# Group norm's remainder in the first chunk, two products exchanged, low-rank products two units later

## The chip, the cores and the metric

The kernel runs on one core of a Trainium2 chip. The metric is the device time of one execution in microseconds (us). A core has a matrix engine (PE in the profile; PEld is its loading of weights), a vector engine (DVE), a scalar engine (ACT), a general engine (POOL) and a queue that issues transfers (SP). Each engine takes its instructions in the order in which they were queued. The matrix engine writes only to PSUM, which has eight banks; the vector and the scalar engine read results from there.

## The reference

One layer of a hybrid network over 4096 tokens of width 1024: a causal pooling branch and an RWKV-7 branch read the same normalised input through one projection, and both go into one output projection. The change lies in the RWKV branch.

```python
h = _rmsnorm(x, norm_g[l]) * (1.0 + scale[:, None, :]) + shift[:, None, :]
p = h @ w_in[l]
...
seg = seg + (prev - seg) * mu_shift[l].astype(f32)
r, w_lo, k, v, a_lo, z = jnp.split(seg, split_idx, axis=-1)
w_raw = w0[l] + jnp.tanh(w_lo) @ w_up[l].astype(f32)        # low-rank product 1
w_raw = -jax.nn.softplus(-w_raw) - 0.5
decay = jnp.exp(-jnp.exp(w_raw))
a = jax.nn.sigmoid(a0[l] + a_lo @ a_up[l].astype(f32))      # low-rank product 2
kk = (k * k_k[l]).reshape(B, T, H, N)
kk = kk / jnp.maximum(jnp.linalg.norm(kk, axis=-1, keepdims=True), L2_EPS)
k = k * (1.0 + (a - 1.0) * k_a[l])
yh = _rwkv7_scan(rh, decay, kh, vh, kk, a)                  # S_t = S_{t-1}(diag(w) - kk^T(a kk)) + v^T k
mu = jnp.mean(yh, axis=-1, keepdims=True)
var = jnp.mean(jnp.square(yh - mu), axis=-1, keepdims=True)
yh = (yh - mu) * lax.rsqrt(var + GN_EPS)                    # group norm
yh = yh * ln_w[l].reshape(H, N) + ln_b[l].reshape(H, N)
bonus = jnp.sum(rh * kh * r_k[l].reshape(H, N), axis=-1, keepdims=True) * vh
y_rwkv = (yh + bonus).reshape(B, T, D_RWKV) * jax.nn.silu(z)
```

## The kernel before

A first phase (8 stretches of 512 tokens) makes the pooling branch and writes the normalised input to memory. The second phase, which the change is in, walks over 16 blocks of 256 tokens; a block has four chunks of 64 tokens and eight heads in four pairs `p`. A last phase (`project`) makes the output projection, and fills the last block too.

For each block, `scores` (L649) makes the triangular score matrices of the four chunks, `inverse` (L698) inverts their unit triangular parts by a long sequence of small vector instructions (`Wt` L727 and `W` L732, 30 steps of two), and `chain` (L796) carries the state from chunk to chunk. Between these dependent steps `fill(n)` runs `n` units of `front` (L537) of the next block. A unit is one of the eight k-steps of a projection: three matmuls of 257 columns (L557 to L559). A projection (`seg`) is evicted from PSUM by one ACT and one DVE instruction (L561, L562). `front` makes one projection `lo` and then, for each pair `p`, four: `kS`, `rS`, `vS`, `zS`. After `vS` a row of vector instructions (L606 to L615) makes the operands of the scores of the next block and `rk`, the factor of the bonus.

Three kinds of small work are put between the units of a projection, by the list `mid`, whose key is the unit before which one of them is taken:

- `lowrank` (L588), key 3, so in `vS(p)`: two products `pl`, `pa` (L591, L592), three ACT instructions, the DVE scan `L` (L596), and two exponentials (L597, L598). What is made of `vS(p)` by L608 and later needs these.
- `cent` (L622), key 6: `v` is centred and transposed, `vps` (L625), and copied by two ACT instructions (L627). It needs `vS(p)` alone.
- `bonus` (L632), key 6: a product `pb` of `rk` (L634) and a DVE multiplication `bon` (L635). It needs `rk(p)`.

`cent(p)` is taken in `kS(p+1)`, `bonus(p)` in `rS(p+1)`. Those of the last pair stay over: they and `norms` (L637, the norms of the keys) make the list `todo`, from which `scores` takes one in each of the chunks 0, 1 and 3. In chunk 2 it makes `d2` of the norms.

All these results lie in one pool of PSUM, `ps_pj`, of three banks: `kS`, `vps`, `rS`, `pb`, `vS`, `pl`, `pa`, `zS` follow one another in it, and a product waits until the reader of an earlier one has set a bank free. The scores, the transposed group norm result and the transposed keys (`btp`, L719) share another pool of two banks, `ps_sc`.

The group norm of half a block, `gn` (L868), has three parts: squares, variance and a power on POOL (L871 to L876); `y` times that (L878); and `gn_out` (L885): four transposes `ytp` (L890), four ACT instructions (L892), two DVE instructions (L893, L894) and the transfer of `mx`. For the first half they are spread over chunk 2 of `chain`; for the second half the first part runs at the end of `chain`, the second after chunk 0 of the next block's `scores`, and the third after chunk 2.

The order of the instructions is the written one only in part. A planner at compile time takes, for each engine, what it believes ready, the earlier written first and some parts (`high_priority`: the steps of the inverse, the copies `xa` L822 and `UV` L835, the state's update L849) ahead of others. The matmuls of `chain` and the first one of a projection behind them are pinned to the written order (`ordered`, `unpin`).

Of the kernel before, what the change touches and what calls it, by code (L numbers as in the profile page):

```python
# [52 lines left out]
def kernel(  # L53
# [426 lines left out]
    with ExitStack() as ph:  # L480
# [56 lines left out]
        def front(b, f):  # L537
# [7 lines left out]
                    hx += [ht[:, k, :] for k in range(4)]  # L545


            mid = {3: [], 6: []}

            def seg(m, name, bufs=2):  # L550
                pp = ps_pj.tile([P, TB2 + 1], F32, tag="pj", name=f"pj{b}_{m}")
# [25 lines left out]
            for p in range(NPAIR):  # L577
# [19 lines left out]
                    A.activation(Pp[:, :, 1:], c3(L), AF.Exp, bias=0.0, scale=cexp)  # L597
                    A.activation(Pi, L, AF.Exp, bias=0.0, scale=-cexp)  # L598

                mid[3].append(lowrank)  # L600
                yield
                vS = yield from seg(3 + 4 * p, "vS")
                if p == 0:
# [36 lines left out]
                        PE.matmul(pn[32 * q : 32 * q + 32, :], hsel, sqs[q], start=True, stop=True)  # L640
                    A.copy(ssb, pn)

                mid[6] += [cent, bonus]
                if p < NPAIR - 1:
                    yield
            f["todo"] = [norms] + mid[6]
# [2 lines left out]
        def scores(b, f, fill):  # L649
            AR, BK = f["AR"], f["BK"]  # L650

            d2 = sm.tile([64, NI], F32, tag="d2", name=f"d2_{b}")
            d2T = sm.tile([P, 32], F32, tag="d2T", name=f"d2T{b}")
            sc = blk.tile([P, NI, P], F32, tag="sc", name=f"sc{b}")
            BT = blk.tile([P, NCH, 512], F32, tag="BT", name=f"BT{b}")
            stg = f["stg"] = f["UV"][0:64].rearrange("q c e -> q (c e)")[:, 0:1024].rearrange("q (t i) -> q t i", t=32)
            for ch in range(NCH):

                pts = [pool.tile([P, 512], F32, tag=tg, name=f"scp{b}_{ch}_{tg}") for pool, tg in ((ps_sc, "sc"), (ps_x, "px"))]
                for j in range(4):  # L660
                    for hq in range(2):
                        o = 64 * hq
                        PE.matmul(  # L663
                            pts[hq][:, j * P : (j + 1) * P],
                            BK[o : o + 64, j, ch].rearrange("q a t -> q (a t)"),
                            AR[o : o + 64, j, ch].rearrange("q a t -> q (a t)"),
                            start=True, stop=True,
                        )
                for hq in range(2):
                    V.tensor_mul(  # L670
                        sc[:, ch * NH : (ch + 1) * NH, :].rearrange("q (j h) t -> q j h t", h=2)[:, :, hq],
                        pts[hq].rearrange("q (j t) -> q j t", j=4),
                        mask.unsqueeze(1).to_broadcast([P, 4, P]),
                    )

                for kb in range(2):
                    o, i8 = 32 * kb, slice(ch * NH, (ch + 1) * NH)
                    A.copy(stg[o : o + 32, :, i8], sc[o : o + 32, i8, o : o + 32].rearrange("q i t -> q t i"))  # L678
                fill(FS + 1)
                if ch == 2:  # L680
                    pt = ps_sc.tile([P, 512], F32, tag="sc", name=f"d2p{b}")
                    for c_ in range(NCH):
                        PE.transpose(pt[:64, c_ * P : (c_ + 1) * P], ssb[:, c_ * C : (c_ + 1) * C], ident)
                    V.tensor_scalar_max(
                        d2.rearrange("q (c p h) -> q c p h", c=NCH, h=2),
                        pt[:64].rearrange("q (c p e) -> q c p e", c=NCH, e=32)[:, :, :, 0:2], L2_EPS * L2_EPS,
                    )
                    V.reciprocal(d2, d2)
                    for g in range(2):
                        V.transpose(d2T[64 * g : 64 * g + 64], d2)  # L690
                if ch != 2:
                    f["todo"].pop(0)()
                fill(FS)
                if ch % 2 == 0:
                    run(gns[0], 1)
            f["sc"], f["BT"], f["d2T"] = sc, BT, d2T

        def inverse(b, f, fill):  # L698
# [217 lines left out]
        def run(g, n=100000):  # L916
            for _ in range(n):
                if next(g, run) is run:
                    return
# [48 lines left out]
        gns = [iter(())]  # L968
        fs = {0: {}}
        run(front(0, fs[0]))  # L970
        for b in range(NB2):
            f = fs[b]
            nf = fs[b + 1] = {}
            gf = front(b + 1, nf) if b + 1 < NB2 else iter(())
            fill = lambda n, gf=gf: run(gf, n)
            scores(b, f, fill)
            if b == NB2 - 1:
                gp = itertools.chain(*(project(q) for q in range(NB2)))
                fill = lambda n: run(gp, math.ceil(n * PF))
            inverse(b, f, fill)  # L980
            chain(b, f, fill)
            run(gf)
            if b + 2 == NB2 or NB2 == 1:
                load_wo()
# [68 lines left out]
```

## Time and profile before

| | us |
|---|---|
| time, median of 3 runs | 2112.47 (2110.7 to 2113.29) |
| the profiled execution's own time | 2114.03 |
| its span, first to last instruction | 2112.3 |
| first scores of block 0 to those of block 15 | 447.7 to 1711.8 |
| one block, three lengths in turn | 83.5, 84.6, 84.6 |
| PE busy, share of the span | 94% |
| DVE busy | 66% |
| ACT busy | 50% |
| granted PE clock, mean | 0.984 |

A matmul's duration in the trace includes the time in which it is pipelined with its neighbours, so a row of 257 columns shows 0.27 us while the next one starts 0.11 us later. Busy time of PE is therefore no measure of what it could do; what counts are the waits between the matmuls, and the distance of their starts. A granted clock of 1.00 is 2.4 GHz and one of 0.5 is 1.2 GHz.

### The profile page before, as it was taken

The numbers are of one execution on the slowest core, as the hardware profiler recorded it, in microseconds if no ns is written. First come the engines' busy times: TensorE is split into PE (matmuls) and PEld (weight loads), VectorE is DVE, ScalarE is ACT, GpSimd is POOL, SyncE is SP. The second block draws the span as 40 slices with busy tenths as digits, with TensorE's granted clock in tenths as the row PEclk, the third lists the DMA queues.
The fourth block names the chain that finished last, engine by engine and source line by source line (L and its number), as shares of the span: only waits on it lengthen the run. The fifth ranks groups of instructions, "written<-read, shape, count | busy, mean of one in ns | idle before, by whom it ended". The sixth has DMA issues, their size and how long they took to land.

```text
span 2112.3 us, 48406 instructions
## 1 busy us (share of the span) xinstructions
PE 1979.8 (94%) x20186; PEld 1460.1 (69%) x20186; DVE 1404.4 (66%) x3533; ACT 1045.7 (50%) x2247; POOL 130.8 (6%) x262
## 2 busy tenths in 40 slices
PE   5999999999999999999999999999999989999998
PEld 2444444687777777777777777777777767788886
DVE  7898987466857757668577676685675766533333
ACT  3555433355565565655655656556556553322211
POOL 0000000000000000000000000000000000100000
PEclk8999999999999999999999999999999999999999
DMA  8867767200110110101101101011011334433422
GB/s 311 277 224 240 241 216 271 68 21 2 32 32 2 31 27 7 32 4 30 32 2 31 27 7 32 3 30 32 2 31 31 131 112 139 165 136 133 155 96 74
DMA packets 140445, 183.20 MB, mean 87 GB/s; under 512 B 12097, under 2 KB 94017, under 8 KB 140226
## 3 DMA queue, kind: packets, MB, share of 16 engines
q1 hardware_dynamic: 140226, 180.11, 25.9%
q8 instruction: 158, 2.59, 0.5%
q14 instruction: 61, 0.50, 0.1%
HBM read 121.22 MB, written 58.85 MB: 85 GB/s over the span
## 4 chain that ended last, share of the span: by engine, by line
PE 47%; DVE 31%; ACT 13%; issue 4%; DMA 2%; POOL 1%; SPq 0%; ACTq 0%; DVEq 0%; POOLq 0%
PE po L953 6%; PE po L955 6%; PE po L954 6%; DVE Wt L727 5%; DVE W L732 4%; PE pp L412 4%; PE pp L411 4%; PE pp L410 4%; PE pj L557 3%; PE pj L558 2%; PE pj L559 2%; DVE sc L670 2%; PE scp_sc L663 2%; DVE L L596 2%; ACT UV L678 2%
## 5 line engine op out<-in xcount | busy, mean ns | idle before, releaser
L557 PE MATMUL pj<-hh,w2h 128*128 128x257 f16 x2176 | 604.3, 278 | 14.3 <-DVE kS L562 13.5
L559 PE MATMUL pj<-hh,w2l 128*128 128x257 f16 x2176 | 598.1, 275 | 0.0
L558 PE MATMUL pj<-hl,w2h 128*128 128x257 f16 x2176 | 596.6, 274 | 0.0
L557 PEld LDWEIGHTS <-w2h 128*128 128x128 f16 x2176 | 213.1, 98 | 69.1 <-issue 27.4
L558 PEld LDWEIGHTS <-w2h 128*128 128x128 f16 x2176 | 215.6, 99 | 47.8 <-issue 17.0
L559 PEld LDWEIGHTS <-w2l 128*128 128x128 f16 x2176 | 211.7, 97 | 31.7
L953 PE MATMUL po<-wo,mh 128*128 128x512 f32 x512 | 204.6, 400 | 2.4 <-ACT mh L937 2.4
L954 PE MATMUL po<-wo,mh 128*128 128x512 f32 x512 | 202.1, 395 | 0.0
L411 PE MATMUL pp<-lo,w1h 128*128 128x512 f16 x512 | 194.0, 379 | 1.4 <-DVE lo L225 1.4
L410 PE MATMUL pp<-hi,w1h 128*128 128x512 f16 x512 | 194.1, 380 | 0.6 <-ACT hi L224 0.6
L412 PE MATMUL pp<-hi,w1l 128*128 128x512 f16 x512 | 194.0, 379 | 0.0
L957 DVE TENSOR_TENSOR x<-po,x 128x512 f32<-128x512 f32 x64 | 44.2, 691 | 155.8 <-PE po L955 155.7
L959 ACT ACTIVATE sq<-x 128x512 f32<-128x512 f32 x64 | 40.4, 631 | 212.0 <-DVE x L957 194.9
L727 DVE TENSOR_TENSOR Wt<-W,Ab 128x30 f32<-128x30 f32 (+7 forms) x480 | 118.5, 247 | 13.7 <-ACT Ab L711 3.1
L732 DVE TENSOR_TENSOR W<-W,Wt 128x30 f32<-128x30 f32 (+7 forms) x480 | 117.9, 246 | 8.8
L953 PEld LDWEIGHTS po<-wo,mh 128*128 128x128 f32 x512 | 97.0, 189 | 24.6 <-ACT mh L937 2.6
L954 PEld LDWEIGHTS po<-wo,mh 128*128 128x128 f32 x512 | 96.8, 189 | 22.2
L678 ACT COPY UV<-sc 32x256 f32<-32x256 f32 x128 | 81.5, 637 | 48.4 <-DVE sc L670 46.3
L955 PE MATMUL po<-wo,ml 128*128 128x512 f32 x256 | 101.6, 398 | 0.0
L562 DVE SCALAR_TENSOR_TENSOR kS<-pj,c,kS 128x256 f32<-128x256 f32 x64 | 30.2, 471 | 103.4 <-ACT kS L561 102.9
L412 PEld LDWEIGHTS <-w1l 128*128 128x128 f16 x512 | 50.1, 98 | 61.6 <-issue 2.0
L410 PEld LDWEIGHTS <-w1h 128*128 128x128 f16 x512 | 50.2, 98 | 59.0 <-issue 0.8
(244 smaller groups left out, 3815.1 us busy)
## 6 DMA issues: line engine op xcount, KB each, us to landing
x<-in_x_dram SPq DMA_DIRECT2D x64, 256.0 KB, 3.1
out_dram<-x SPq DMA_DIRECT2D x64, 256.0 KB, 2.0
xk<-in_xT_dram SPq DMA_DIRECT2D x56, 256.0 KB, 4.1
xt<-in_x_dram SPq DMA_DIRECT2D x28, 512.0 KB, 5.7
wada<-in_w_ada_dram SPq DMA_DIRECT2D x24, 512.0 KB, 6.7
w2raw<-in_w_in_dram SPq DMA_DIRECT2D x17, 512.0 KB, 6.0
hh<-hT_hi SPq DMA_DIRECT2D x32, 257.0 KB, 4.1
hl<-hT_lo SPq DMA_DIRECT2D x32, 257.0 KB, 3.3
```

Of the source, the lines that this page charges most:

```text
L410: PE.matmul(pp, w1_hi[m][:, k, :], hi, start=(k == 0), stop=False)
L411: PE.matmul(pp, w1_hi[m][:, k, :], lo, start=False, stop=False)
L412: PE.matmul(pp, w1_lo[m][:, k, :], hi, start=False, stop=(k == KT - 1))
L557: unpin(PE.matmul(pp, w2_hi[m][:, k, :], hh[k], start=(k == 0), stop=False))
L558: PE.matmul(pp, w2_hi[m][:, k, :], hl[k], start=False, stop=False)
L559: PE.matmul(pp, w2_lo[m][:, k, :], hh[k], start=False, stop=(k == KT - 1))
L678: A.copy(stg[o : o + 32, :, i8], sc[o : o + 32, i8, o : o + 32].rearrange("q i t -> q t i"))
L727: V.tensor_mul(tmp[:, :n, :k], W[:, r0:, k : k + 1].to_broadcast([P, n, k]), Ab[:, k : k + 1, :k].to_broadcast([P, n, k]),)
L732: V.tensor_add(W[:, r0:, :k], W[:, r0:, :k], tmp[:, :n, :k])
L953: unpin(PE.matmul(po, mh[:, k, ts_], wo[0][k][n], start=(k == 0), stop=False))
L954: PE.matmul(po, mh[:, k, ts_], wo[1][k][n], start=False, stop=False)
L955: PE.matmul(po, (ml[:, k] if b % 2 == 0 else ml[k])[:, ts_], wo[0][k][n], start=False, stop=(k == KT - 1))
```

## The change

The low-rank products are taken before unit 5 of `vS` and not before unit 3. `bonus` and `cent` change places, so that `bonus(p)` is taken in `kS(p+1)` and `cent(p)` in `rS(p+1)`, and in `todo` the last pair's bonus stands before its `cent`. `scores` takes two of `todo` (`norms` and the bonus) in chunk 0, one (`cent`) in chunk 1 and none later. After chunk 0 the group norm runs to its end, so that its third part moves from chunk 2 to chunk 0.

```diff
-            mid = {3: [], 6: []}
+            mid = {5: [], 6: []}
...
-                mid[3].append(lowrank)
+                mid[5].append(lowrank)
...
-                mid[6] += [cent, bonus]
+                mid[6] += [bonus, cent]
...
-                if ch != 2:
+                for _ in range((2, 1, 0, 0)[ch]):
                     f["todo"].pop(0)()
                 fill(FS)
-                if ch % 2 == 0:
-                    run(gns[0], 1)
+                if ch == 0:
+                    run(gns[0])
```

## Rows read from the trace of the kernel before

**Rows 1.** The page's first part: each engine's busy us, share, instructions.
```profile
PE 1979.8 (94%) x20186; PEld 1460.1 (69%) x20186; DVE 1404.4 (66%) x3533; ACT 1045.7 (50%) x2247; POOL 130.8 (6%) x262
```

**Rows 2.** Windows, two blocks: length; busy PE, PEld, DVE, ACT, POOL; granted clock; DMA, GB/s.
```profile
1288.20:1372.80 84.60, 78.81 (x1061) 62.63 (x1060) 58.61 (x167) 50.08 (x116) 5.94 (x11) 0.98 0.08 21
1372.80:1456.40 83.60, 77.78 (x1062) 61.87 (x1061) 58.59 (x167) 49.98 (x116) 5.94 (x11) 1.00 0.08 22
```

**Rows 3.** Waits of PE, blocks 0 to 14: us in total, times, longest.
```profile
PE psn L843 <- ACT UV L835: 24.9, 15, 1.7
...
PE btp L719 <- ACT BT L720: 17.4, 15, 1.2
PE pj L557 <- DVE kS L562: 13.5, 14, 1.0
...
PE pa L592 <- DVE rS L562: 13.0, 29, 0.5
...
PE pl L591 <- DVE bon L635: 8.8, 29, 0.3
```

**Rows 4.** Timeline around chunk 2 of `chain`: start, us, instruction, [idle before, releaser].
```profile
1363.23 0.69 DVE L878 TENSOR_TENSOR y<-y,rstd 128x512 f32<-128x512 f32 x1 [1.75 <-POOL rstd L876]
1363.84 0.68 DVE L596 TENSOR_TENSOR_SCAN L<-rst,tw 128x256 f32<-128x256 f32 x1
...
1364.55 0.42 ACT L597 ACTIVATE Ppad<-L 128x256 f32<-128x256 f32 x1 [1.59 <-DVE L L596]
...
1365.18 0.73 ACT L835 COPY UV<-psn 64x256 f32<-64x256 f32 x2
...
1365.96 0.69 PE L843 MATMUL psn<-UV,BT 128*64 128x64 f32 x16 [1.66 <-ACT UV L835]
```

**Rows 5.** Windows: the stretch behind that wait, columns as in rows 2.
```profile
1367.80:1370.40 2.60, 2.60 (x41) 1.79 (x40) 1.69 (x5) 2.12 (x6) 0.00 (x0) 0.53 0.00 0
```

**Rows 6.** Timeline of PE: the low-rank products of pair 3, in `chain`.
```profile
1361.00 0.48 PE L591 MATMUL pl<-lo,up 64*128 64x256 f32 x1
1361.01 0.48 PE L592 MATMUL pa<-lo,up 64*128 64x256 f32 x1
...
1361.63 0.28 PE L557 MATMUL pj<-hh,w2h 128*128 128x257 f16 x1
```

**Rows 7.** Timeline of PE: the low-rank products of pairs 0 and 1.
```profile
1309.79 0.70 PE L591 MATMUL pl<-lo,up 64*128 64x256 f32 x2
1310.86 0.70 PE L592 MATMUL pa<-lo,up 64*128 64x256 f32 x2 [0.38 <-DVE rS L562]
...
1323.49 0.70 PE L591 MATMUL pl<-lo,up 64*128 64x256 f32 x2 [0.32 <-DVE bon L635]
1324.71 0.70 PE L592 MATMUL pa<-lo,up 64*128 64x256 f32 x2 [0.52 <-DVE rS L562]
```

**Rows 8.** Timeline: pair 0's scan and `rk`, then `vps` of pairs 0, 1.
```profile
1312.73 0.68 DVE L596 TENSOR_TENSOR_SCAN L<-rst,tw 128x256 f32<-128x256 f32 x1
...
1317.77 0.48 DVE L615 SCALAR_TENSOR_TENSOR rk<-rS,pv,ta 128x256 f32<-128x256 f32 x1
...
1317.81 0.61 PE L625 MATMUL vps<-cmat,vS 128*128 128x128 f32 x4
...
1331.66 0.61 PE L625 MATMUL vps<-cmat,vS 128*128 128x128 f32 x4
```

**Rows 9.** Timeline of `scores`: chunk 1's first product; `y`; group norm's sum; chunk 3's copies.
```profile
1293.31 0.37 PE L663 MATMUL scp_sc<-AR,BK 64*128 64x128 f32 x1
...
1294.14 0.69 DVE L878 TENSOR_TENSOR y<-y,rstd 128x512 f32<-128x512 f32 x1 [0.23 <-POOL rstd L876]
...
1301.61 0.69 DVE L893 TENSOR_TENSOR mx<-mx,bon 128x512 f32<-128x512 f32 x1 [1.77 <-ACT mx L892]
...
1304.13 1.28 ACT L678 COPY UV<-sc 32x256 f32<-32x256 f32 x2 [2.56 <-DVE sc L670]
```

**Rows 10.** Windows: the inverse, columns as in rows 2; timeline: its last transpositions.
```profile
1305.40:1338.10 32.70, 29.47 (x241) 24.11 (x241) 31.07 (x98) 17.26 (x38) 1.64 (x7) 1.00 0.01 3
...
1334.31 2.11 DVE L745 STREAM_TRANSPOSE UV<-W 64x512 f32<-64x512 f32 x2
```

## The prediction

> **What bounds the kernel now.** I read the page first: PE is busy for 94% of the span, no other engine for more than 66% [rows 1]. So PE is the engine to watch, and what can be gained is its waits. The windows of two neighbouring blocks show how regular the second phase is: 84.6 and 83.6 us with the same instructions, the longer one at a mean clock of 0.98 and the shorter at 1.00 [rows 2]. Then the list of PE's waits over blocks 0 to 14: the same few waits come once in each block [rows 3]. Per block they are 1.66 us before the product L843 of chunk 2 (24.9 by 15), 1.16 us before a `btp` (17.4 by 15), 0.97 us before `vS(2)` (13.5 by 14), and about 0.45 us for each `pa` of pairs 0 and 1 and 0.30 us for each `pl` of pairs 1 and 2. The change touches the neighbourhood of every one of them. I therefore went to the timeline around each, and last to the inverse, where DVE is busy for 31.07 of 32.7 us [rows 10]: there PE can't run ahead of DVE by much, whatever is taken out of its way.
>
> The sum is per block and times 15 (blocks 0 to 14 run with a `front` between their steps). It is made against the profiled execution's 2114.03 us, of which 2112.3 is the span and 1.7 lies around it; the median of the runs is 2112.47, so 1.6 comes off at the end.
>
> **Low-rank products, chain (pair 3).** Today they lie before the product L827 of chunk 2. The chain of the 1.66 us wait is written out in [rows 4]: `y` waits for the power on POOL, the scan stands behind `y` on DVE, ACT waits 1.59 us for the scan in front of the exponential L597, and the copy `UV` L835, whose input has been there, is queued behind that exponential; PE's L843 waits for the copy. Two units later the products come behind L827, since the five units before unit 5 are used up by then. The copies L835 are then ready before `tw` and `ta` exist, and stand ahead of the exponentials. What is late next is the scan itself, which now lies beside the state's update L849 and the copies of the next step. I take 1.4 of the 1.66 (bounds 0 and 1.66).
>
> The wait has a second price. In the stretch behind it the granted clock is 0.53 for 2.6 us [rows 5], the lower of the two levels (1.2 GHz), and matmuls that start every 0.11 us elsewhere start at half that pace. In every third block it stays high: that is the difference of 84.6 and 83.6 [rows 2]. Two blocks of three times 1.0 are 0.7 per block, which go with the wait.
>
> **Low-rank products, pairs 0 to 2, and the bonus one projection earlier.** These two must be taken together. Today pair 0 needs 1.07 us from `pl` to `pa`, since `pa` waits for `rS` to leave its bank, and pair 1 0.32 and 1.22 [rows 7]. Where both banks are free, as in pair 3, the two products run side by side and cost 0.63 in all (1361.00 to 1361.63) [rows 6]. Two units later both banks should be free. If nothing else came in, pair 0 would save 1.07 and pair 1 1.22 + 0.32 = 1.54.
>
> But the bonus needs `rk`, `cent` doesn't. For pair 0, counted from the place where `pl` stands now (1309.79): `vps` starts at 8.02, which is 1.07 + 0.63 + 19 units of 0.333 [rows 7, 8]. After the change the same place is reached at 0.67 (two units) + 0.63 + 17 x 0.333 = 6.96, and `pb` stands there. `rk` ends 5.52 after the scan begins (1312.73 to 1318.25), and the scan begins 1.87 after `pa` [rows 7, 8]; with the products at 0.67 that is 0.67 + 1.87 + 5.52 = 8.06. So `pb` waits 1.1 us for `rk`, and the place is passed at 8.06 where it is 8.02 now: nothing gained. In pair 1 the place is 1331.66 - 1323.49 + 0.32 = 8.49 now [rows 7, 8], and 8.06 after: 0.43 gained. Pair 2's bonus falls into the chain, long after its `rk`. Together 0.4 less. The bounds are 2.6 less, if the planner lets units pass the waiting `pb`, and 1.75 more, if `rk` ends 0.67 later than it does now (9.13 against 8.02 and 8.49).
>
> The waiting `pb` holds up everything behind it on PE, the units above all. The Trainium skill (TensorE: Matmul & The Clock Gate, Part 3) says that matmuls start and end strictly in the order of the queue. No row here shows one passing another that waits, so the trace agrees; only the planner's order at compile time could let the units pass, and by the rule the wait of 1.1 us is paid in full where it places `pb` early.
>
> In pair 2, `vS` waits 0.97 for `kS`, whose eviction stands behind the transpositions L745 (2.11 us) [rows 3, 10], and `pl` 0.30. `vS` will have the bank of the bonus to choose as well, and the inverse begins earlier (next part), so the transpositions fall earlier against PE. I take 0.8 less of 1.27; both ends stay open, since DVE is full there.
>
> **Group norm and the bonus in `scores`.** Chunk 3 now pays for the third part in chunk 2: the sum L893 waits 1.77 for ACT in front of chunk 3's masks, the copies L678 of chunk 3 wait 2.56 for those masks, and the copies of `btp` stand behind them on ACT [rows 9]; hence the 1.16 us of `btp`. With the third part in chunk 0, chunk 3 has only its own masks, so I take 1.0 less (bounds 0 and 1.16; the copy L711 of the inverse, now earlier, may come in between). In chunk 0, `y` ends at 1294.83, while PE is at chunk 1's first product at 1293.31 [rows 9]: up to 1.5 us of waiting for the four transposes, if they are queued ahead of chunk 1. The 1.77 of L893 moves too, and can hold chunk 1's masks; behind those PE has three units (1.0) before chunk 2 wants a bank, so up to 0.8. I take 0.6 more between 0 and 2.3, near the low end, since the planner has chunk 1's products to put ahead. The work itself only changes its place. The bonus of pair 3 in chunk 0 has its `rk` since the chain and frees its bank before `cent` in chunk 1. On SP the store of `mx` moves forward with the third part, and stands behind the loads of the next `front`, with nothing queued that waits for it. POOL's queue keeps its order.
>
> **The sum.** -1.4 - 0.7 - 0.4 - 0.8 - 1.0 + 0.6 = -3.7 per block, times 15 is -55.5: 2058.5 against the profiled execution, 2057 against the median.
>
> **The rivals.**
> 1. The planner lets units pass `pb`, so pairs 0 and 1 gain their 2.6: -5.9 per block, 2024. For it: it orders by what it believes ready. Against it: its belief may run ahead of the chip, where `pl` and `pa` were queued 0.3 to 0.5 too early [rows 7].
> 2. The chain's wait only changes its place: the scan, later now, holds `y`'s copies or `xa` instead of `UV`, and the clock falls as before. -0.4 there in place of -2.1: 2082.
> 3. Slower: `rk` slips. DVE is at 95% in the inverse [rows 10], and a scan that comes two units later ends `rk` 0.67 later than now. Then `pb` waits 9.13 - 6.96 = 2.17 in pairs 0 and 1, longer than the 1.66 after which the clock fell [rows 4, 5], so that 0.7 more goes in each. Pairs 0 and 1 give +1.75 + 1.4 in place of -0.4, pair 2's 0.8 is lost with DVE's delay: +0.65 per block, 2122. It decides from about 2 us of wait at each `pb`; with `scores` at its bad end too it is 2148.
> 4. The changed text does not change the queues where it matters (the planner floats the steps back to where their inputs are ready), or gains and losses cancel: 2112.
>
> **How the numbers follow.** Forecast 2057 with 0.55 (its own range 2035 to 2080), rival 1 0.15, rival 2 0.12, rival 3 0.13, rival 4 0.05. Faster by over 0.2% (4 us, about what a measurement of this kernel can tell) is 0.82, within it 0.05, slower 0.13. The range reaches from below rival 1, whose bounds go on to 2012, to 2108; rival 3 and most of rival 4 lie outside.
>
> **What would show it.** Right: L843 of chunk 2 starts without a wait for L835 and no block shows the clock of 0.53 behind it; all `pl` and `pa` pairs at 0.63; the second `btp` wait gone; `pb` of pairs 0 and 1 waiting about 1 us for `rk`; blocks of about 80.6 us. Wrong: waits of over 2 us at `pb`; transposes or masks in chunk 0 and 1 that hold PE by more than 1 us; new waits at `xa` or S in chunk 3; a changed order of the planner anywhere that brings waits the trace of before doesn't have.

## The result, and the profile after

| | before | after |
|---|---|---|
| median time, us | 2112.88 (4 runs) | 2144.72 (2139.36 to 2145.66) |
| ratio to before, 95% interval | | 1.0146 (1.0126 to 1.0165) |
| the profiled execution's own time, span | 2114.03, 2112.3 | 2145.66, 2143.9 |
| mean block, first scores of block 0 to those of block 15 | 84.28 | 86.54 |

The change makes the kernel 1.5% slower; 2057 us had been forecast, with 2108 as the upper end. The engines' totals tell nothing of it; the first part of the page after:

```profile
PE 1994.5 (93%) x20186; PEld 1469.6 (69%) x20186; DVE 1413.7 (66%) x3533; ACT 1041.4 (49%) x2247; POOL 126.4 (6%) x262
```

The list of PE's waits over blocks 0 to 14 does (us in total, times, longest); it answers to [rows 3]:

```profile
PE qp L756 <- DVE MQ L746: 48.8, 15, 3.3
PE pb L634 <- DVE rk L615: 25.6, 15, 1.7
PE psn L827 <- ACT xa L822: 8.7, 30, 0.4
PE pa L592 <- DVE rS L562: 5.3, 15, 0.4
PE ytp L890 <- DVE y L878: 4.9, 14, 0.4
...
PE psn L843 <- ACT UV L835: 0.4, 1, 0.4
```

The waits of [rows 3] are nearly all gone: before L843 24.9 us have become 0.4, and those before `btp` and before `vS` of pair 2 are not in the list. In their place stand 48.8 us before `qp`, 3.25 per block, and 25.6 us before `pb`, 1.7 per block. The first of these no rival had named.

The timeline of block 5 shows what `qp` waits for. First PE (start, us, instruction, idle before, releaser), then DVE in the same stretch:

```profile
921.80 0.28 PE L559 MATMUL pj<-hh,w2l 128*128 128x257 f16 x1
925.32 0.43 PE L756 MATMUL qp<-MQ,sc 32*32 32x32 f32 x26 [3.24 <-DVE MQ L746]
925.78 0.45 PE L634 MATMUL pb<-rk,bones 128*128 128x256 f32 x1
```

```profile
920.66 0.69 DVE L743 TENSOR_TENSOR W<-W,d2T 128x512 f32<-128x512 f32 x1
921.26 0.42 DVE L610 TENSOR_TENSOR ta<-ta,kS 128x256 f32<-128x256 f32 x1
921.60 2.07 DVE L745 STREAM_TRANSPOSE UV<-W 64x512 f32<-64x512 f32 x2
923.70 0.43 DVE L612 TENSOR_TENSOR BK<-ta,Pi 128x256 f32<-128x256 f32 x1
924.04 1.23 DVE L746 STREAM_TRANSPOSE MQ<-UV 32x1024 f32<-32x1024 f32 x1
925.20 0.43 DVE L615 SCALAR_TENSOR_TENSOR rk<-rS,pv,ta 128x256 f32<-128x256 f32 x1
925.56 0.47 DVE L562 SCALAR_TENSOR_TENSOR zS<-pj,c,zS 128x256 f32<-128x256 f32 x1
925.96 0.46 DVE L562 SCALAR_TENSOR_TENSOR kS<-pj,c,kS 128x256 f32<-128x256 f32 x1
```

The closing steps of the inverse (L743 to L746) hold DVE from 920.66 to 925.27, with two short instructions of pair 1 (L610, L612) between them, and the eviction of `zS` of pair 1, then that of `kS` of pair 2, come behind them. `kS(2)` is complete on PE at about 922.1, and the next projection has no bank. The planner has filled the hole with the first 26 products of `qp`, which need the last of the closing steps. The same stretch of DVE in the kernel before, a part that [rows 10] cut short:

```profile
1331.58 0.48 DVE L615 SCALAR_TENSOR_TENSOR rk<-rS,pv,ta 128x256 f32<-128x256 f32 x1
...
1332.08 0.47 DVE L562 SCALAR_TENSOR_TENSOR zS<-pj,c,zS 128x256 f32<-128x256 f32 x1
...
1333.38 0.68 DVE L743 TENSOR_TENSOR W<-W,d2T 128x512 f32<-128x512 f32 x1
...
1336.46 0.48 DVE L562 SCALAR_TENSOR_TENSOR kS<-pj,c,kS 128x256 f32<-128x256 f32 x1
```

There `rk(1)` and the eviction of `zS(1)` come before L743. Only `kS(2)` stands behind a part of the closing steps, and it is wanted one projection later; that was the 0.97 us before `vS(2)` [rows 3], a wait that is gone after the change.

Counted from the first score product of block 5, in us (unit n is the n-th unit queued on PE in the block; unit 82 begins `rS(2)`):

| | before | after | difference |
|---|---|---|---|
| inverse begins (L709) | 17.25 | 16.48 | -0.77 |
| unit 30 | 23.64 | 21.72 | -1.92 (the low-rank products not yet done) |
| unit 48 | 30.06 | 29.48 | -0.58 |
| unit 50 (after pair 0's wait) | 30.73 | 32.52 | +1.80 |
| unit 80 | 43.91 | 43.67 | -0.23 |
| closing steps begin (L743) | 45.17 | 43.08 | -2.09 |
| unit 82 | 44.57 | 48.71 | +4.14 |
| unit 110 (start of the chain) | 60.35 | 63.31 | +2.96 |
| next block's first scores | 83.53 | 85.27 | +1.74 |

Up to unit 80 the change is worth 0.23 us; between units 80 and 82, 4.37 us are lost; behind it some 2.4 come back, where pair 2 waited before and in the chain. Of the 4.37, 3.24 are the wait. Most of the rest is work that stands there now, the 26 products of `qp` and `pb`, and stood elsewhere before.

### The profile page after: what moved, and what is told of

The parts are those of the page before. It is cut to its first block, busy times and chain, and to the rows that moved or that the text cites. A ratio compares the mean times of both kernels' runs of the same rounds, so it can differ in the third digit from the quotient of the medians.

```text
span 2143.9 us, 48451 instructions
## 1 busy us (share of the span) xinstructions
PE 1994.5 (93%) x20186; PEld 1469.6 (69%) x20186; DVE 1413.7 (66%) x3533; ACT 1041.4 (49%) x2247; POOL 126.4 (6%) x262
## 4 chain that ended last, share of the span: by engine, by line
PE 49%; DVE 29%; ACT 9%; issue 9%; DMA 2%; POOL 1%; SPq 0%; ACTq 0%; POOLq 0%; DVEq 0%
PE po L953 6%; PE po L955 5%; PE po L954 5%; DVE W L732 5%; DVE Wt L727 5%; PE pp L412 4%; PE pp L411 4%; PE pp L410 4%; PE pj L557 3%; PE pj L558 3%; PE pj L559 3%; DVE L L596 2%; DVE sc L670 2%; PE pb L634 2%; PE psn L827 2%
## 5 line engine op out<-in xcount | busy, mean ns | idle before, releaser
L562 DVE SCALAR_TENSOR_TENSOR rS<-pj,c,rS 128x256 f32<-128x256 f32 x64 | 30.8, 481 | 136.0 <-ACT rS L561 136.0
```

## The experiments

The difference has three parts, so I first ran each part and each pair of parts alone. The parts are L (low-rank products at unit 5), X (the exchange) and G (group norm and the list `todo`).

**L with G: `low_gn`.** The changed kernel with

```diff
-                mid[6] += [bonus, cent]
+                mid[6] += [cent, bonus]
```

> The changed kernel with the exchange alone undone: the centring comes first again, the bonus one projection later; low-rank products at unit 5 and group norm in chunk 0 stay. Theory A (the bonus stands ahead of its factor rk, and the two long waits of PE, 1.78 us before pair 0's bonus product and 3.32 us before the early part of qp, both come from that): both waits go, the gains at L843, btp and vS(2) stay, about 80.7 us per block and 2060 us. Rival B (the planner pulls qp forward because the inverse begins earlier with group norm in chunk 0, whatever the bonus does): the 3.3 us stay, only the 1.78 goes, about 2118 us. Rival C (the low-rank products two units later are what delays the rest): no faster than 2130 us.

Measured: 2139.16 us, 1.0122 (1.0105 to 1.0139). Theory A falls: without the exchange the kernel is nearly as slow. Rival B's wait before `qp` is there, though the time is 21 us above its figure, and rival C's bound is met as well; the next runs tell these two apart. PE's waits:

```profile
PE qp L756 <- DVE MQ L746: 45.5, 15, 3.0
PE pj L557 <- DVE zS L562: 18.2, 15, 1.2
```

And in place of the bonus product, the projection `rS(1)` waits 1.2 us, for the eviction of `zS` of pair 0.

**L with X: `low_swap`.** The changed kernel with

```diff
-                for _ in range((2, 1, 0, 0)[ch]):
+                if ch != 2:
                     f["todo"].pop(0)()
                 fill(FS)
-                if ch == 0:
-                    run(gns[0])
+                if ch % 2 == 0:
+                    run(gns[0], 1)
```

> The changed kernel with group norm and the list todo as before (third part in chunk 2, one of todo in chunks 0, 1 and 3); low-rank products at unit 5 and the exchange stay. Theory A: the bonus still stands ahead of rk, so PE still waits some 5 us per block for it, and the btp wait of 1.2 us comes back for the 0.5 us at the transposes: about 2150 us. Rival B (earlier inverse): the 3.3 us before qp are gone, about 2105 us. Rival C: as now, about 2145 us.

Measured: 2098.83 us, 0.9926 (0.9909 to 0.9942). Near rival B's figure: without G the kernel is faster than before, though `pb` still waits (28.0 us put down to `rk` and 21.1 us to the steps of the inverse queued around it). Theory A and rival C had it as slow as the whole change.

**`qp` kept in place: `after_qp_pinned`.**

```diff
-                    PE.matmul(pt[32 * q : 32 * q + 32, j * 32 : (j + 1) * 32], sc[0:32, i, 32:64], MQ[0:32, i, :], start=True, stop=True)
+                    ordered(PE.matmul(pt[32 * q : 32 * q + 32, j * 32 : (j + 1) * 32], sc[0:32, i, 32:64], MQ[0:32, i, :], start=True, stop=True))
```

> The changed kernel with the 32 matmuls of qp (L756) pinned to the written order on PE, so that none of them is queued ahead of the units written before it. Theory A: the 3.3 us are pair 1's bonus product waiting for rk, with qp only standing in front of it; it waits for rk itself now, and the time is within 15 us of the changed kernel's, 2130 to 2145 us. Rival B: qp queued early is itself the wait, which goes: 3.3 us less per block, about 2095 us.

Measured: 2150.81 us, 1.0176 (1.0161 to 1.0191). No faster than the change, and far from rival B's 2095: `qp` queued early only stands in front of the hole. The wait passes to the bonus product, whose `rk` is behind the closing steps too, as theory A had it; the next run shows that `rk` is not the last thing in the way.

```profile
PE pb L634 <- DVE rk L615: 77.6, 29, 3.7
```

**No wait for `rk`: `after_bonus_no_rk`.** The bonus term of the output is left out by it.

```diff
-                    PE.matmul(pb, bones, rk, start=True, stop=True)
+                    PE.matmul(pb, bones, vS, start=True, stop=True)
```

> The changed kernel with the bonus product reading vS in place of rk: the same instructions of the same size, but nothing waits for rk (the bonus term of the output is left out so). Theory A: neither the 1.78 us before pair 0's bonus product nor the 3.3 us before qp are left, about 2060 us. Rival B: only the first goes, about 2118 us. Rival C: the waits for pa and the late scan stay, no faster than 2130 us.

Measured: 2140.13 us, 1.0126 (1.0111 to 1.0141). With nothing waiting for `rk` the time hardly falls. The wait before `qp` is 45.7 us in 15 blocks, 3.05 each, and the wait of pair 0 has become one for the eviction of `zS` (18.3 us, 15 times). In block 5, `rS(2)` then starts at 48.35 from the block's first scores, and the eviction of `zS(1)` ends at 48.30. So the bonus is not what holds the kernel; both waits are for work that is late on DVE.

**Each part alone.** `only_low`, `only_swap` and `only_gn` are the kernel before with the lines of L, X or G; `swap_gn` has X and G.

> The kernel before with one part of the change: low-rank products before unit 5. Theory A (only the exchange does harm): the 1.9 us before L843 of chunk 2 and most of the clock lost behind it go, and pl and pa wait less: about 3 us less per block, 2068 us. Rival C (the later low-rank products do the harm): slower than before, about 2130 us.

Measured: 2077.36 us, 0.9835 (0.9819 to 0.9852), which no run beats beyond its interval, and within 10 us of the expectation. The wait before L843 is gone and every block takes 82.0 us.

> The kernel before with one part of the change: bonus and centring exchanged (in the list todo too). Theory A: pairs 0 and 1 wait for rk, about 0.5 to 1.5 us each, with the low-rank products still at unit 3, and the other waits stay: about 2135 us. Rival B (harm only together with the earlier inverse): within 10 us of before, 2113 us.

Measured: 2132.85 us, 1.0096 (1.0079 to 1.0113), near theory A's figure, with waits of 0.37 and 0.43 at `pb` and longer ones at the low-rank products.

> The kernel before with one part of the change: group norm's remainder in chunk 0, and the list todo taken two, one, none, none (its order stays centring, then bonus). Theory A: the btp wait of 1.2 us goes and 0.5 us at the transposes comes, about 2103 us. Rival B (the earlier inverse makes the planner queue qp too early): a new wait before qp, about 2140 us.

Measured: 2125.01 us, 1.0058 (1.0042 to 1.0074): slower, though the `btp` wait is gone. The new wait is not at `qp` but at `rS(2)`, for the eviction of `zS`:

```profile
PE pj L557 <- DVE zS L562: 27.0, 15, 1.8
```

> The changed kernel with the low-rank products back before unit 3; exchange and group norm in chunk 0 stay. Theory A: rk ends two units earlier, so the bonus waits are smaller but there, and the 1.9 us before L843 and the clock lost behind it come back: about 2135 us. Rival C (the later low-rank products do the harm): no slower than before, about 2105 us.

Measured: 2123.41 us, 1.0051 (1.0036 to 1.0066), between the two expectations.

So L alone gains, and G costs in three companies of four: 1.0058 alone, 1.0122 against 0.9835 beside L, 1.0146 against 0.9926 beside L and X; beside X alone it is 1.0051 against 1.0096. All the kernels with G have a wait at unit 82, none of those without it has. That gave theory D: G lets the inverse begin 0.77 us earlier and end earlier still, and its closing steps, which have priority, get ahead of the evictions. The next four runs test it.

**Closing steps without priority: `after_tail_plain`.** The changed kernel with

```diff
             MQ = blk.tile([P, NI, 32], F32, tag="Ab", name=f"MQ{b}")
-            with tc.high_priority(offset=PRI):
+            if True:
                 for kb in range(2):
...
                 V.tensor_mul(W, W, d2T.unsqueeze(1).to_broadcast([P, 16, 32]))
```

> The changed kernel with the closing steps of the inverse (L743 to L748: a product, three transpositions, a copy) at ordinary priority and not ahead of all else. Theory D, formed from the runs so far (group norm in chunk 0 lets the inverse end some 2 us earlier, and its closing steps, 4.6 us on DVE, are now queued ahead of the evictions of zS of pair 1 and kS of pair 2 and of rk of pair 1; PE has no bank and waits 3.3 us): the evictions go first, the 3.3 us wait goes, about 2095 us. Rival E (the wait is for the result of the inverse itself, which PE reaches too early): the result comes later still, so the wait stays or grows, no faster than 2140 us.

Measured: 2085.62 us, 0.9867 (0.9851 to 0.9884): 59 us faster than the change, and faster than before. Per mean block that is 4.04 us (86.54 against 82.50). In block 5, whose clock is full in both, it is 2.58; the rest is for the most part the lower clock of other blocks, which is gone: every block behind block 0 takes 82.7 to 83.0. The DVE timeline of block 5 shows the new order; `rk` and `zS` come between L743 and the transpositions:

```profile
902.57 0.69 DVE L743 TENSOR_TENSOR W<-W,d2T 128x512 f32<-128x512 f32 x1
903.51 0.48 DVE L615 SCALAR_TENSOR_TENSOR rk<-rS,pv,ta 128x256 f32<-128x256 f32 x1
903.91 0.48 DVE L562 SCALAR_TENSOR_TENSOR zS<-pj,c,zS 128x256 f32<-128x256 f32 x1
904.30 1.05 DVE L745 STREAM_TRANSPOSE UV<-W 64x512 f32<-64x512 f32 x1
905.96 1.06 DVE L745 STREAM_TRANSPOSE UV<-W 64x512 f32<-64x512 f32 x1
907.05 0.48 DVE L562 SCALAR_TENSOR_TENSOR kS<-pj,c,kS 128x256 f32<-128x256 f32 x1
907.45 1.22 DVE L746 STREAM_TRANSPOSE MQ<-UV 32x1024 f32<-32x1024 f32 x1
```

`MQ` comes 1.8 us later than in the changed kernel (49.52 against 47.69 from the block's first scores) and `qp` does not wait for it, so rival E falls.

**The inverse held back: `after_inv_late`.** The changed kernel with

```diff
             with tc.high_priority(offset=PRI):
+                for _ in range(2):
+                    V.tensor_mul(Ab[0:64], f["stg"], f["stg"])
                 V.transpose(Ab[0:64], f["stg"])
```

> The changed kernel with two further DVE products of 64 x 1024 (some 2.4 us of DVE work, whose result is overwritten) ahead of the inverse's first transposition, so that the inverse begins and ends later as it did before. Theory D: more work, but the closing steps fall behind the eviction of zS of pair 1 again; the 3.3 us go, about 1.3 us before vS of pair 2 come back: about 2115 us. Rival E: DVE is the bound in this stretch and the result comes later, so the time grows by up to 2.4 us per block, 2145 to 2180 us.

Measured: 2102.82 us, 0.9955 (0.9941 to 0.9970). More work, on the engine that is fullest there, and 42 us less than the changed kernel. It is also 12 us less than expected: the closing steps fall behind `kS(2)` too, so the wait before `vS(2)` does not come back. The lines behind the insertion are numbered two higher: L745 is the product, L747 and L748 the transpositions.

```profile
911.77 0.48 DVE L615 SCALAR_TENSOR_TENSOR rk<-rS,pv,ta 128x256 f32<-128x256 f32 x1
912.29 0.48 DVE L562 SCALAR_TENSOR_TENSOR zS<-pj,c,zS 128x256 f32<-128x256 f32 x1
914.27 0.48 DVE L562 SCALAR_TENSOR_TENSOR kS<-pj,c,kS 128x256 f32<-128x256 f32 x1
915.17 0.69 DVE L745 TENSOR_TENSOR W<-W,d2T 128x512 f32<-128x512 f32 x1
916.12 2.12 DVE L747 STREAM_TRANSPOSE UV<-W 64x512 f32<-64x512 f32 x2
```

**Without priority, L alone: `low_tail_plain`.** The same edit in the kernel before with L.

> The kernel before with low-rank products at unit 5 and the closing steps of the inverse at ordinary priority. Theory D: the wait of 1.4 us before vS of pair 2, whose bank stands behind the same closing steps, goes: about 2058 us against 2077 of the low-rank products alone. Rival E: no faster than 2077 us.

Measured: 2077.28 us, 0.9830 (0.9815 to 0.9844), no different from L alone. The expectation missed here: `kS(2)` is evicted at 48.03 in both, since the planner puts the same order on DVE with and without the priority. The wait before `vS(2)` stays (18.8 us, 15 times, so 1.25 and not 1.4 each).

**Which line of G: `low_swap_gnpart`.** The changed kernel with `todo` taken as before.

```diff
-                for _ in range((2, 1, 0, 0)[ch]):
+                if ch != 2:
                     f["todo"].pop(0)()
```

> The changed kernel with the list todo taken as before (one in each of the chunks 0, 1 and 3), so that of the last part only group norm's move to chunk 0 is left. Theory D: the move alone frees chunk 3's masks and copies and lets the inverse begin earlier: 2135 to 2150 us, as the whole change. Rival F (the bonus in chunk 0, not group norm, is what shifts the inverse): about 2099 us, as without the third part.

Measured: 2139.95 us, 1.0130 (1.0115 to 1.0145). Group norm's move alone is enough. The inverse begins at 16.65 here. The `btp` wait is still there (19.1 us, 15 times), so that wait was not a matter of group norm alone, as the prediction had it; where `todo` is taken in chunks 0 and 1 alone as well (`only_gn`, the changed kernel) it is gone.

**What is left without the collision.** Two more runs have the closing steps without priority, and L and G, or G alone.

> The changed kernel with the exchange undone and the closing steps of the inverse at ordinary priority. If the exchange costs what its waits show once the closing steps are out of the way (1.78 and 1.22 us before the bonus products of pairs 0 and 1, of which some is given back as waits for a bank, as the pair of runs with the low-rank products alone and with the exchange added shows: about 1 us per block): about 2070 us, the fastest so far. If these waits only stand in for waits for DVE that come anyway: 2085 us, as with the exchange.

Measured: 2086.04 us, 0.9868 (0.9851 to 0.9884), the same as with the exchange (0.9867). With G the exchange costs nothing by itself: its waits stand in for others. L alone is 9 us faster than L with G, so the move costs a little even so. Against L alone, PE is 0.15 us ahead at unit 30 in place of the forecast 0.4, loses 0.66 at pair 0's low-rank products, where `pa` waits for `rS` again (5.6 us in 15 blocks) and the two no longer overlap, and loses 0.73 more at unit 82.

> The kernel before with group norm's remainder in chunk 0 (and todo two, one, none, none) and the closing steps of the inverse at ordinary priority. Theory D: the wait of 2.0 us before rS of pair 2 goes, and what is left of the move is its forecast gain (btp wait gone, 0.5 us at the transposes): 2095 to 2105 us against 2125 with the closing steps ahead. Rival: the move itself costs time, 2120 us or more.

Measured: 2110.40 us, 0.9986 (0.9977 to 0.9995), against 1.0058 with the priority. The wait at unit 82 goes; the forecast gain of the move hardly shows. The `btp` wait (17.4 us before) is gone, but the waits for `rS` before `pa` grow from 13.0 to 22.8 us, and the transposes wait 4.7.

The runs in one table, from block 5 of each profile, in us from its first score product, ordered by ratio (`zS(1)` evicted: start of its DVE instruction):

| kernel | ratio | L745 begins | `zS(1)` evicted | unit 80 to unit 82 |
|---|---|---|---|---|
| `low_tail_plain` | 0.9830 | 45.90 | 43.22 | 0.66 |
| `only_low` | 0.9835 | 45.91 | 43.22 | 0.67 |
| `after_tail_plain` | 0.9867 | 45.15 | 44.75 | 0.66 |
| `low_gn_tail_plain` | 0.9868 | 45.09 | 44.69 | 1.39 |
| `low_swap` | 0.9926 | 46.07 | 43.39 | 0.67 |
| `after_inv_late` | 0.9955 | 48.76 | 44.93 | 0.66 |
| `gn_tail_plain` | 0.9986 | 45.33 | 44.00 | 0.66 |
| before | 1 | 46.11 | 43.88 | 0.66 |
| `swap_gn` | 1.0051 | 44.58 | 46.71 | 1.94 |
| `only_gn` | 1.0058 | 44.58 | 46.70 | 2.63 |
| `only_swap` | 1.0096 | 46.09 | 43.86 | 0.67 |
| `low_gn` | 1.0122 | 43.97 | 47.94 | 4.12 |
| `after_bonus_no_rk` | 1.0126 | 43.86 | 47.83 | 4.63 |
| `low_swap_gnpart` | 1.0130 | 43.41 | 48.48 | 4.81 |
| after | 1.0146 | 44.02 | 47.98 | 5.04 |
| `after_qp_pinned` | 1.0176 | 44.03 | 48.00 | 5.53 |

Wherever the transpositions L745 begin before `zS(1)` is evicted, the two units take 1.9 to 5.5 us where 0.66 is their work; wherever they begin after it, 0.66 to 1.39. Of the slower kernels only `only_swap` has another cause.

The table names DVE, but the closing steps end in a copy on ACT (L747), which has the same priority and waits for L745. ACT in block 5 of `low_gn`, then DVE and PE:

```profile
920.82 1.04 ACT L747 COPY UV<-UV 32x1024 f32<-32x1024 f32 x1 [2.88 <-DVE UV L745]
921.89 0.74 ACT L627 COPY UV<-vps 64x256 f32<-64x256 f32 x2
922.66 0.47 ACT L561 ACTIVATE kS<-pj,c 128x256 f32<-128x256 f32 x1
```

```profile
922.68 0.47 DVE L562 SCALAR_TENSOR_TENSOR zS<-pj,c,zS 128x256 f32<-128x256 f32 x1
```

```profile
922.71 0.39 PE L557 MATMUL pj<-hh,w2h 128*128 128x257 f16 x1
```

The copies of `vps` and ACT's half of the eviction of `kS(2)` stand behind L747. `rS(2)` starts right after the copies of `vps`, and 0.44 us before `zS(1)` has left its bank; so in this kernel it was ACT that set the bank free. In the changed kernel, too, ACT's half of `kS(2)` stands behind L747. `after_tail_plain` and `after_inv_late` change the order on both engines: that the closing steps hold PE up is shown, how much of it goes by DVE and how much by ACT is not.

## Why the prediction was wrong

**The step that failed** is the last of the part on pairs 0 to 2: "the inverse begins earlier (next part), so the transpositions fall earlier against PE. I take 0.8 less". The premise was right: the inverse begins 0.77 earlier and its closing steps 2.09 earlier. The sign was wrong. I looked only at the projection that the transpositions hold up now (`kS(2)`, wanted by `vS(2)`) and saw them leave it. I did not look at what they meet when they come earlier: `rk(1)` and the eviction of `zS(1)`, which pass just ahead of them before (1332.08 against 1333.38). In place of 0.8 saved, PE waits 3.24 at unit 82; the waits of 0.97 and 0.30 in pair 2 did go. The wait of 0.97 [rows 3] was the visible edge of this collision, and I took it for something that could only get smaller; "both ends stay open" was written beside it, without a price for the bad end.

**The sum, term by term.** Per block, with block 5 for the waits: `scores` (up to unit 28) -0.11 where -0.4 was forecast, pairs 0 to 2 (to unit 112, where the chain has begun) +2.62 for -1.2, the chain -0.77 for -1.4, and the clock +0.52 for -0.7, since the mean block stands 1.27 above block 5 after the change and 0.75 before. Together +2.26 in place of -3.7. Two terms have the wrong sign, and the collision is not all of the first. In `after_tail_plain`, without it, pairs 0 to 2 stand at +0.47, with 42.8 us in 30 waits of `pb` for `rk`. In `only_low`, without the exchange too, they stand at -0.3: the low-rank products overlap, in part, but PE waits 1.2 us before `rS(1)` for the eviction of `zS(0)` and 1.27 before `vS(2)`, and 0.6 more are lost between units 108 and 110. The prediction had said that PE can't run ahead of DVE by much here, and set nothing off for it.

**The chain** was right. The wait of 1.66 before L843 [rows 4] is gone. L alone shows it undisturbed: in block 5, whose clock is full before too, the stretch from unit 112 to the block's end is 1.24 us shorter, where 1.4 were forecast; and all its blocks take 82.0, so that the 0.75 by which the mean block stood above block 5 before (84.28 against 83.53) is gone as well, where 0.7 were forecast. A remnant of rival 2 is left in the changed kernel, some 0.3 us twice a block before L827 for `xa`, and with it the chain gains 0.77 there.

**The bonus waiting for `rk`** happened, at 1.7 us in pair 0 where 1.1 were worked out. `pa` waited for `rS` once more (0.35, as the 0.38 of [rows 7]), and the scan began 3.72 us after `pl`, where 1.87 had been counted from the pair's start. But the wait is not a cost of its own. Where it is taken away (`after_bonus_no_rk`), or the exchange undone (`low_gn`), a wait for a bank takes its place. Only without G does the exchange cost, 0.9 to 1.0%.

**`scores`.** The `btp` wait went and the transposes wait 0.35, so these two figures are close to the forecast, but their sum, 0.4 forecast, shows as 0.11 at units 22 to 28. A little less PE time in `scores` was traded for an inverse that begins at a worse moment.

**The rivals.** The slower one was forecast at 2122 to 2148 and 2144.72 came, but its mechanism did not: it had `rk` slipping by two units in both pairs and the clock falling behind each `pb`. `rk(1)` did slip, by 4.19 us (43.86 to 48.05), behind the closing steps, and not because the scan came later by itself. That a changed order of the planner could bring new waits was said, as a thing that would show the prediction wrong, and had no share in the chances.

What stays open is the 9 us between L and L with G once the collision is gone. The rows name the places (pair 0's `pa`, unit 82), and no run separates them.

## What to carry to other kernels

An engine that is full in a stretch is not relieved by moving a high-priority block on it earlier: ask which instructions pass just ahead of that block now, and who waits for them when it overtakes them. A short wait at such a place can be the edge of a collision, whose bad end is set by the whole block (4.6 us here, of which PE waited 3.24), not by the wait (0.97). And parts of a change should be summed with the queue order that they make together: L gains 1.65% alone and 0.74% with X, and loses 1.22% with G.

## What the runs showed of the hardware

A wait of the same length has two prices. In the changed kernel PE waits 3.25 us before `qp` in every block. In block 5 the granted clock behind it stays at 1.00, and the block takes 85.3 us; in block 8 it falls to 0.50 for the next stretch, and the block takes 88.3 (windows: length, busy PE, PEld, DVE, ACT, POOL, granted clock, DMA, GB/s):

```profile
918.00:926.00 8.00, 4.73 (x64) 3.92 (x63) 7.92 (x21) 3.21 (x6) 1.37 (x4) 1.00 0.01 2
926.00:930.00 4.00, 4.00 (x36) 3.48 (x36) 1.51 (x5) 1.94 (x5) 0.00 (x0) 1.00 0.00 0
```

```profile
1180.00:1184.00 4.00, 0.75 (x25) 0.45 (x26) 3.95 (x7) 1.52 (x2) 0.79 (x1) 0.93 0.00 0
1184.00:1188.00 4.00, 4.00 (x39) 2.80 (x30) 1.92 (x6) 0.90 (x2) 0.15 (x1) 0.50 0.00 0
```

The wait is 3.24 to 3.26 us long in all fifteen blocks; in the 4 us behind it the clock is 1.00 in five of them (3 to 6 and 12) and lower in ten. So 3 us of a block's time can hang on nothing that these rows show of the block itself. The forecast had treated it as a fixed share of blocks, two in three as in [rows 2], at 1.0 us each. The share is two in three again, though not in turn; the price is not: behind block 0 a block with the lower clock takes 86.8 to 88.3 us, the others 85.3.
